# Batch normalization on one core: the first tile's store goes out in two transfers

## The chip, the cores and the metric

The kernel runs on one core of a Trainium2 chip. The metric is the device time of one execution in microseconds (us). Before the change the median of 3 runs is 2484.38 us (2483.38 to 2485.73).

## What is computed

The input `x` is 32 x 256 x 128 x 128 in float32, 536.9 MB. Each of the 256 channels has its own `gamma`, `beta`, `running_mean` and `running_var`:

```python
eps = 1e-5
out = gamma * (x - running_mean) / sqrt(running_var + eps) + beta   # per channel
```

That is one multiplication and one addition per element, `x * scale + shift`, with `scale = gamma / sqrt(var + eps)` and `shift = beta - mean * scale`. Every element is read once from HBM and written once to HBM.

## The kernel before

**Tiles.** A tile holds 128 channels of one image: 128 partitions, each with one row of 128 x 128 = 16384 floats (64 KB). There are 32 x 2 = 64 tiles of 8.4 MB. Three buffers `t0` to `t2` hold them in rotation; tile i lies in buffer i modulo 3 and is transformed in place.

**Queues.** Loads are issued by SyncE (`load`, line 86; its queue is SP, the DMA queue q1). Stores are issued by ScalarE (`store`, line 89; its queue is ACT's, the DMA queue q10). Both queues feed the same 16 DMA engines. Each engine moves 8 of the 128 rows of a tile.

**Start.** Tile 0 is loaded in two halves with the four parameter loads between them (line 103); loads 1 and 2 are issued right behind, as their buffers are free. The parameters are turned and combined into `scale_t` and `shift_t` (lines 108 to 125).

**Loop.** For each tile VectorE transforms the first columns (`apply_vector`, line 66) and ScalarE the rest (`apply_scalar`, line 77). Tile 0 is split in half at column 8192. For the other tiles VectorE does columns 0 to 1696, then 1696 to 14976, and ScalarE the last 1408; the last tile has other bounds. Then the store of the tile is issued.

**What sets the order.** The instructions of each engine stand in the order in which the code writes them (`manual_schedule`); waits follow from what each reads and writes. A load into a buffer waits until the store from that buffer has landed: load i+1 waits for store i-2. `follow` adds two more waits by hand:

- Load i+1 waits for VectorE's first piece of tile i, so that a load starts when the load before has landed.
- ScalarE's piece of tile i (for 0 < i < 62) waits for the store of tile i-1 to land. As store i comes after that piece, one store at a time is under way. `stored` is the transfer it waits for.

The loop writes these as

```python
if NHEAD <= i + 1 < NT:
    follow(load(i + 1), released)
...
part = apply_scalar(i, VHEAD if i == 0 else VLAST if i == last else VMOST, HW)
if 0 < i < NT - 2:
    follow(part, stored)
stored = store(i)
```

Of the kernel before, what the change touches and what calls it, by code (L numbers as in the profile page):

```python
# [1 line left out]

# [4 lines left out]


NBUF = 3
PAD = 936  # L10
NHEAD = 3
VFIRST = 1696
VMOST = 14976
VHEAD = 8192
VLAST = 9216


@with_exitstack
def kernel(
    ctx: ExitStack,  # L20
    tc: tile.TileContext,
    x: bass.AP,
    gamma: bass.AP,
    beta: bass.AP,
    running_mean: bass.AP,
    running_var: bass.AP,
    out: bass.AP,
):
    nc = tc.nc
    eps = 1e-5  # L30
    f32 = mybir.dt.float32

    N, C, H, W = x.shape
    P = nc.NUM_PARTITIONS
    assert C % P == 0
    NCB = C // P
    HW = H * W
    NT = N * NCB
    B = 32
    NQ = P // B  # L40
    NE = 16
    NPAR = 4

    xr = x.rearrange("n (cb p) h w -> (n cb) p (h w)", p=P)
    outr = out.rearrange("n (cb p) h w -> (n cb) p (h w)", p=P)

    params = ctx.enter_context(tc.tile_pool(name="params", bufs=1))
    data = ctx.enter_context(tc.tile_pool(name="data", bufs=1))
    params.tile([P, PAD], f32, name="pad", tag="pad")
    bufs = [data.tile([P, HW], f32, name=f"t{s}", tag=f"t{s}") for s in range(NBUF)]  # L50
    rows = params.tile([B, NPAR * C], f32, name="rows", tag="rows")
    turned = params.tile([B, NPAR * C], f32, name="turned", tag="turned")
    par = params.tile([P, NPAR, NCB], f32, name="par", tag="par")
    eps_t = params.tile([P, 1], f32, name="eps_t", tag="eps")
    std_t = params.tile([P, NCB], f32, name="std_t", tag="std")
    rstd_t = params.tile([P, NCB], f32, name="rstd_t", tag="rstd")
    scale_t = params.tile([P, NCB], f32, name="scale_t", tag="scale")
    ms_t = params.tile([P, NCB], f32, name="ms_t", tag="ms")
    shift_t = params.tile([P, NCB], f32, name="shift_t", tag="shift")

    left, right = slice(0, HW // 2), slice(HW // 2, HW)
    last = NT - 1

    def apply_vector(i, first_col, end):
        t, cb = bufs[i % NBUF], i % NCB
        return nc.vector.tensor_scalar(  # L66
            out=t[:, first_col:end],
            in0=t[:, first_col:end],
            scalar1=scale_t[:, cb : cb + 1],
            scalar2=shift_t[:, cb : cb + 1],  # L70
            op0=mybir.AluOpType.mult,
            op1=mybir.AluOpType.add,
        )

    def apply_scalar(i, first_col, end):
        t, cb = bufs[i % NBUF], i % NCB
        return nc.scalar.activation(  # L77
            out=t[:, first_col:end],
            in_=t[:, first_col:end],
            func=mybir.ActivationFunctionType.Identity,  # L80
            bias=shift_t[:, cb : cb + 1],
            scale=scale_t[:, cb : cb + 1],
        )

    def load(i, rows=slice(0, P), cols=slice(0, HW)):
        return nc.sync.dma_start(out=bufs[i % NBUF][rows, cols], in_=xr[i][rows, cols])  # L86

    def store(i, rows=slice(0, P), cols=slice(0, HW)):
        return nc.scalar.dma_start(out=outr[i][rows, cols], in_=bufs[i % NBUF][rows, cols])

    def follow(inst, ahead):
        tc.add_manual_dep(
            inst.ins,
            ahead.ins.name,
            mybir.DependencyInfo(mybir.DependencyClass.Sync, mybir.DependencyReason.DATA),
            reason="one transfer at a time in each queue, released by the computation",
        )

    with tc.manual_schedule():
        load(0, cols=left)  # L100
        nc.vector.memset(rows[:], 0.0)  # L101
        for r, ap in enumerate((running_var, gamma, beta, running_mean)):
            nc.sync.dma_start(out=rows[0:NE, r * C : (r + 1) * C], in_=ap.partition_broadcast(NE))  # L103
        load(0, cols=right)
        for i in range(1, NHEAD):
            load(i)

        nc.vector.memset(eps_t[:], eps)  # L108
        nc.vector.transpose(out=turned[:], in_=rows[:])  # L109
        blocks = turned.rearrange("p (rc q b) -> p rc q b", q=NQ, b=B)  # L110
        flat = par.rearrange("p r cb -> p (r cb)")
        for q in range(NQ):
            nc.vector.tensor_copy(out=flat[q * B : (q + 1) * B], in_=blocks[:, :, q, 0])  # L113
        var_t, gamma_t, beta_t, mean_t = (par[:, r] for r in range(NPAR))
        nc.scalar.activation(  # L115
            out=std_t[:],
            in_=var_t,
            func=mybir.ActivationFunctionType.Sqrt,
            bias=eps_t[:],
            scale=1.0,  # L120
        )
        nc.vector.reciprocal(out=rstd_t[:], in_=std_t[:])  # L122
        nc.vector.tensor_mul(out=scale_t[:], in0=gamma_t, in1=rstd_t[:])  # L123
        nc.vector.tensor_mul(out=ms_t[:], in0=mean_t, in1=scale_t[:])  # L124
        nc.vector.tensor_sub(out=shift_t[:], in0=beta_t, in1=ms_t[:])  # L125

        stored = None
        for i in range(NT):
            if i == 0:
                apply_vector(i, 0, VHEAD)  # L130
            else:
                released = apply_vector(i, 0, VFIRST)
                if NHEAD <= i + 1 < NT:
                    follow(load(i + 1), released)
                apply_vector(i, VFIRST, VLAST if i == last else VMOST)
            part = apply_scalar(i, VHEAD if i == 0 else VLAST if i == last else VMOST, HW)
            if 0 < i < NT - 2:
                follow(part, stored)
            stored = store(i)


# [1 line left out]
_INS = ['x', 'gamma', 'beta', 'running_mean', 'running_var']  # L143
_OUTS = [((32, 256, 128, 128), 'float32')]


# [23 lines left out]
```

## Time and profile before

| | us |
|---|---|
| median of 3 runs | 2484.38 |
| the profiled execution, whole | 2483.26 |
| its span on the core | 2481.2 |
| VectorE busy | 526.0 |
| ScalarE busy | 111.9 |
| VectorE idle, waiting for loads (line 66) | 1915.2 |
| ScalarE idle, waiting for stores (line 77) | 2271.7 |

The span runs from the first instruction to the last event on the core; the 2.1 us between it and the whole execution lie outside. HBM is read for 536.94 MB and written for 536.87 MB, 433 GB/s over the span. In the timeline a row names its start, its length, the engine ("ACTq" and "SPq" are the queues of ScalarE and SyncE, where transfers are issued), the line and the operation; in brackets stands how long the engine was idle before it and what released it. The landing of a load is read from the VectorE row that it releases, the landing of a store from the ScalarE row. The trace also holds a record of every DMA packet: start, length, bytes, queue.

### The profile page before, as it was taken

Reading aid. Unit: us, or ns where it says so; the run is one execution under the profiler, and the core shown is the slowest. Engines: PE = TensorE matmul, PEld = TensorE weight load, DVE = VectorE, ACT = ScalarE, POOL = GpSimd, SP = SyncE. Lnnn points to the kernel's source line nnn. Section 1 sums busy time; section 2 is a strip of 40 time slices with the busy share of each in tenths; the row PEclk is TensorE's granted clock in tenths of the full one; section 3 lists DMA queues with packets and bytes.
Section 4 is the critical chain, followed back from the end, with each engine's and each line's share of the span. In section 5 each row is a group of like instructions: output and inputs, shape, how many; then the busy total and the mean of one; then the engine's idle time right before and its main releaser. Section 6 shows DMA issues by size and latency. Waiting matters only on the chain.

```text
span 2481.2 us, 695 instructions
## 1 busy us (share of the span) xinstructions
DVE 526.0 (21%) x138; ACT 111.9 (5%) x66; POOL 0.2 (0%) x4
## 2 busy tenths in 40 slices
DVE  2122121221212212122121221212212212122120
ACT  1000000000000000000000000000000000000001
POOL 0000000000000000000000000000000000000000
DMA  9999999999999999999999999999999999999999
GB/s 422 425 438 437 426 437 436 428 437 440 425 437 438 426 436 438 427 437 438 426 437 438 427 437 437 426 438 437 426 440 437 427 437 437 433 431 437 434 429 408
DMA packets 18709, 1073.86 MB, mean 433 GB/s; under 512 B 2128, under 2 KB 2192, under 8 KB 2192
## 3 DMA queue, kind: packets, MB, share of 16 engines
q1 hardware_dynamic: 9488, 536.94, 50.0%
q10 hardware_dynamic: 9216, 536.88, 49.9%
q14 instruction: 5, 0.04, 0.0%
HBM read 536.94 MB, written 536.87 MB: 433 GB/s over the span
## 4 chain that ended last, share of the span: by engine, by line
DMA 94%; DVE 3%; another core or an unknown queue 1%; ACT 0%; issue 0%; SPq 0%; DVEq 0%
DMA t<-in_x_dram 94%; DVE t L66 3%; ACT t L77 0%; SPq L86 0%; SPq L103 0%; DVEq L66 0%; DVE rows L101 0%; DVE eps_t L108 0%
## 5 line engine op out<-in xcount | busy, mean ns | idle before, releaser
L66 DVE TENSOR_SCALAR t<-t,scale_t,shift_t 128x13280 f32<-128x13280 f32 (+2 forms) x127 | 522.6, 4157 | 1915.2 <-DMA t<-in_x_dram 1915.2
L77 ACT ACTIVATE t<-t,shift_t,scale_t 128x1408 f32<-128x1408 f32 (+1 forms) x64 | 110.3, 1723 | 2329.3 <-DMA out_dram<-t 2271.7
L109 DVE STREAM_TRANSPOSE turned<-rows 32x1024 f32<-32x1024 f32 x1 | 1.2, 1232 | 11.9 <-DMA rows<-in_running_mean_dram 11.9
L115 ACT ACT_TABLE_LOAD x1 | 1.3, 1283 | 0.7 <-PEq L154 0.7
L101 DVE MEMSET rows<- 32x1024 f32 x1 | 0.9, 912 | 1.0 <-PEq L154 1.0
L115 ACT ACTIVATE std_t<-par,eps_t 128x2 f32<-128x2 f32 x1 | 0.3, 295 | 13.8 <-DVE par L113 13.8
L113 DVE COPY par<-turned 32x8 f32<-32x8 f32 x4 | 0.6, 161 | 0.1
L122 DVE RECIPROCAL rstd_t<-std_t 128x2 f32<-128x2 f32 x1 | 0.2, 165 | 0.4 <-ACT std_t L115 0.4
L124 DVE TENSOR_TENSOR ms_t<-par,scale_t 128x2 f32<-128x2 f32 x1 | 0.2, 161 | 0.0
L125 DVE TENSOR_TENSOR shift_t<-par,ms_t 128x2 f32<-128x2 f32 x1 | 0.2, 161 | 0.0
L123 DVE TENSOR_TENSOR scale_t<-par,rstd_t 128x2 f32<-128x2 f32 x1 | 0.2, 160 | 0.0
L154 POOL MEMSET const-bfloat16-1.0<- 128x1 bf16 x1 | 0.1, 102 | 0.0
L154 POOL MEMSET const-uint8-127<- 128x1 uint8 x1 | 0.1, 101 | 0.0
L154 POOL MEMSET const-float32-0.0<- 128x1 f32 x1 | 0.1, 98 | 0.2 <-issue 0.2
L154 POOL MEMSET const-float32-1.0<- 128x1 f32 x1 | 0.1, 98 | 0.0
L108 DVE MEMSET eps_t<- 128x1 f32 x1 | 0.1, 59 | 0.0
## 6 DMA issues: line engine op xcount, KB each, us to landing
t<-in_x_dram SPq DMA_DIRECT2D x2, 4096.0 KB, 15.8
out_dram<-t ACTq DMA_DIRECT2D x64, 37.0
t<-in_x_dram SPq DMA_DIRECT2D x63, 37.3
rows<-in_running_var_dram SPq DMA_DIRECT2D x1, 16.0 KB, 11.2
rows<-in_gamma_dram SPq DMA_DIRECT2D x1, 16.0 KB, 11.0
rows<-in_beta_dram SPq DMA_DIRECT2D x1, 16.0 KB, 10.7
rows<-in_running_mean_dram SPq DMA_DIRECT2D x1, 16.0 KB, 10.4
```

Source lines behind the costliest of these rows:

```text
L66: return nc.vector.tensor_scalar(out=t[:, first_col:end], in0=t[:, first_col:end], scalar1=scale_t[:, cb : cb + 1], scalar2=shift_t[:, cb ...
L77: return nc.scalar.activation(out=t[:, first_col:end], in_=t[:, first_col:end], func=mybir.ActivationFunctionType.Identity, bias=shift_t[: ...
L101: nc.vector.memset(rows[:], 0.0)
L108: nc.vector.memset(eps_t[:], eps)
L109: nc.vector.transpose(out=turned[:], in_=rows[:])
L113: nc.vector.tensor_copy(out=flat[q * B : (q + 1) * B], in_=blocks[:, :, q, 0])
L115: nc.scalar.activation(out=std_t[:], in_=var_t, func=mybir.ActivationFunctionType.Sqrt, bias=eps_t[:], scale=1.0,)
L122: nc.vector.reciprocal(out=rstd_t[:], in_=std_t[:])
L123: nc.vector.tensor_mul(out=scale_t[:], in0=gamma_t, in1=rstd_t[:])
L124: nc.vector.tensor_mul(out=ms_t[:], in0=mean_t, in1=scale_t[:])
L125: nc.vector.tensor_sub(out=shift_t[:], in0=beta_t, in1=ms_t[:])
L154: nc = _bacc.Bacc("TRN2", target_bir_lowering=False, num_devices=1)
```

## The change

The store of tile 0 is issued as two transfers: columns 0 to 1024 (128 rows of 4 KB), then columns 1024 to 16384 (128 rows of 60 KB). The wait of ScalarE's piece of tile 1 follows the second. All other stores stay whole. Lines behind the new constant move down by one.

```diff
+LEAD = 1024
...
-            stored = store(i)
+            if i == 0:
+                store(i, cols=slice(0, LEAD))
+                stored = store(i, cols=slice(LEAD, HW))
+            else:
+                stored = store(i)
```

Columns 0 to 1024 are written by VectorE alone; the second transfer holds columns of VectorE and of ScalarE. Load 3, which goes into the buffer of tile 0, waits for both transfers.

## The prediction

> **What bounds the kernel now.** I read the page's lines of transfer rates, then the timeline of the first tiles and of a late one, then the packet records that lie under the DMA rows of the trace (start, length, bytes and queue of every packet).
>
> ```profile
> span 2481.2 us, 695 instructions
> ...
> DMA  9999999999999999999999999999999999999999
> GB/s 422 425 438 437 426 437 436 428 437 440 425 437 438 426 436 438 427 437 438 426 437 438 427 437 437 426 438 437 426 440 437 427 437 437 433 431 437 434 429 408
> ...
> q1 hardware_dynamic: 9488, 536.94, 50.0%
> q10 hardware_dynamic: 9216, 536.88, 49.9%
> ```
>
> The 16 DMA engines are full in every slice; the loads (q1) and the stores (q10) each take half. The compute engines are nowhere near: DVE is busy 526.0 us, ACT 111.9. The packet records say how full. A row of a tile (65536 bytes) is one packet of 2.414 us; the records form 16 chains, each record ending where the next begins; each chain holds 1032 data packets worth 1024 whole rows, and 1024 x 2.4143 = 2472.2 us. After 20 us I find no gap over 0.05 us in any chain. So 2472.2 of the span's 2481.2 us is moving bytes, and 9.0 us is the rest: 2.1 before the first packet, 0.9 after the last, some 6 of stretched packets. A change can win at most a few us here; it can lose whatever it lets the engines stand empty.
>
> What keeps them full is when the two queues pause:
>
> ```profile
> 0.73 0.37 SPq L86 DMA_DIRECT2D t<-in_x_dram  x1
> ...
> 23.29 7.21 ACT L77 ACTIVATE t<-t,shift_t,scale_t 128x8192 f32<-128x8192 f32 x1 [7.20 <-DMA t<-in_x_dram]
> 30.53 0.38 ACTq L89 DMA_DIRECT2D out_dram<-t  x1
> 52.74 8.27 DVE L66 TENSOR_SCALAR t<-t,scale_t,shift_t 128x1696 f32<-128x1696 f32 x2 [31.29 <-DMA t<-in_x_dram]
> 74.63 1.56 ACT L77 ACTIVATE t<-t,shift_t,scale_t 128x1408 f32<-128x1408 f32 x1 [44.13 <-DMA out_dram<-t]
> 76.22 0.34 ACTq L89 DMA_DIRECT2D out_dram<-t  x1
> 84.39 8.27 DVE L66 TENSOR_SCALAR t<-t,scale_t,shift_t 128x1696 f32<-128x1696 f32 x2 [23.37 <-DMA t<-in_x_dram]
> ...
> 113.91 1.56 ACT L77 ACTIVATE t<-t,shift_t,scale_t 128x1408 f32<-128x1408 f32 x1 [37.72 <-DMA out_dram<-t]
> 115.50 0.34 ACTq L89 DMA_DIRECT2D out_dram<-t  x1
> 123.72 8.27 DVE L66 TENSOR_SCALAR t<-t,scale_t,shift_t 128x1696 f32<-128x1696 f32 x2 [31.06 <-DMA t<-in_x_dram]
> ```
>
> An ACT row starts when the store before has landed (74.63: store 0; 113.91: store 1); a DVE row starts when a load has landed (84.39: load 2; 123.72: load 3). So store i lands 9.8 us **before** load i+2, and late in the run still (ACT 2395.79, DVE 2405.54). In the pause of the stores the loads have the engines, in the pause of the loads the stores. One engine's packets in order (L a load's row, s a store's), from 22.6 us:
>
> ```
> LLLLL sLsLsL ss LsLsLs LLLLL ssss LsLsLsLs LLLL ssss LsLsLsLs
> ```
>
> Four rows of each alone, eight alternating. Two things are seen here. Both queues waiting, they take **turns packet by packet**. And the 4-byte packet that raises the semaphore takes a whole turn: load 1 has its eighth row, a store's row follows, then the load's semaphore packet, then again a store's row: the "ss". Its cost shows too: the last row of load 1 ended at 50.31 us, its last semaphore packet at 52.72, one packet later.
>
> **The change, part by part.** Nothing is removed. Store 0 becomes 128 rows of 4096 bytes and 128 rows of 61440: for each engine 8 small packets, a semaphore packet, 8 large ones, a semaphore packet.
>
> *Added work.* 4 KB at the same rate is 0.15 us, and 8 x 0.15 + 8 x 2.26 is what 8 whole rows took. The parameter rows (1024 bytes) took 46 ns where their bytes make 38, so 8 ns a packet: under 0.1 us for 8. A second issue on ACT's queue costs 0.4 us (30.53 0.38), with nothing behind it but the activation of tile 1, which waits for the store until after 70 us. Nothing.
>
> *An earlier start.* In the order of the changed kernel's instructions the small store waits for the vector half alone, not for the activation ahead of it; the large one waits for the activation. The trace of before shows no issue beside a running ACTIVATE, so it leaves between 23.3 us (when that ACTIVATE starts) and 30.5. I take the early end, since the wait is all that held the store; both lead to the same place below.
>
> *The turns.* This decides. Before, store 0 took 8 turns of rows and one of its semaphore against the loads' turns. Now it takes 8 + 1 + 8 + 1, and 9 of them move nearly nothing. Count for one engine. Load 1's rows begin at 22.5 to 23.3 us. In before, the store issued at 30.53 had its first packet at 35.28 us at the earliest: one load row was still chosen ahead. A lead issued at 23.3 so comes first after two rows of load 1, at 27.3 to 28.1. Load turns left: 6 rows of load 1, its semaphore, 8 rows of load 2: 15. The small rows and their semaphore use 9 of these; the large rows meet the last 6; then come the seventh large row, load 2's semaphore, the eighth large row. So store 0 lands one row, 2.3 us, **after** load 2. With the late issue (first packet at 35.3, 5 rows of load 1 gone) the same count leaves 4 large rows behind load 2's semaphore: 9.1 us after. Before it was 9.8 us ahead. When it lands is fixed by bytes: 8 + 8 + 8 rows from 22.5 to 23.3 us are 24 x 2.414 = 57.9 us, so 80.4 to 81.2, and with the stretch at the first store packet (load rows of 3.1 to 3.6 us near 32 us) up to 82; before, 74.6.
>
> *What is late next.* Load 3 goes into tile 0's buffer, so it waits for store 0; so does the activation of tile 1, by the pacing, and with it store 1. Both queues are empty when store 0 lands, and the engines stand still until load 3's first packet. Load 3 starts at once, store 1 after 1.56 us of ACT. The load so has two rows before the first store row, keeps that lead through the alternation, and lands before store 1. Load 4 waits for store 1 by its buffer, store 2 by the pacing: again one event frees both. Nothing in the loop undoes it, as the load always ends first and always waits. Stores 0 to 60 each release such a pair (loads 3 to 63): **61 pauses**.
>
> *Price of a pause.* No row of before shows an empty engine between tiles. The nearest is the start: issue at 0.73, first packet at 2.11 (1.38 us). The first half rows took 1.8 to 2.0 us where later ones took 1.21, so 0.6 more. From landing to issue 0.1 us (the ACT starts 0.04 us after store 0's last semaphore packet, SP issues 0.06 us after the DVE's release at 85.56). Sum 0.1 + 1.38 + 0.6 = 2.08 us. From below: 0.05 + 1.38 with no slow first row, 1.43. From above: a late load, issued at 2406.78 with its first packet at 2410.72, is 3.94 us less the row chosen ahead (2.41), 1.53; with 0.15 to issue, 0.8 for the slow row, and 0.74 by which the engines' first packets spread at the start (2.11 to 2.85): 3.22. I take 2.08, the start's own rows. A gain has no place in a pause.
>
> *Sum.* 61 x 2.08 = 126.9 us, on the profiled execution's 2483.26 us (span 2481.2 and 2.1 around it; 1.1 below the median 2484.38): 2610.1. Ends: 61 x 1.43 = 87 gives 2570, 61 x 3.22 = 196 gives 2680.
>
> **The rivals.** *The lead takes one turn, not nine.* If an engine passed all 8 small rows at a stroke, store 0 would be delayed by one or two turns at 2.41 us and start up to 7 us earlier: it would land some 5 us or more before load 2, the pauses would lie apart as now, and nothing would stand still: 2483.3, and within 0.2% (5 us, about what a measurement of this kernel can tell from no change). The same holds if turns were shared by bytes, since store 0 then has the bytes it had. For it: no row of before shows small data rows of one queue beside another. Against: whole rows alternate singly, and a packet of 4 bytes took a full turn, at the end of every transfer. It decides if store 0 lands 4 us or more ahead of load 2.
>
> The Trainium skill ("DMA: Bandwidth & Descriptors", section Queues, rings and completion order) speaks for this rival: an engine is to drain a whole packet, typically 9 to 17 descriptors, from one ring before it turns to the next. The lead's 8 rows and semaphore on an engine are 9 descriptors; by that rule they are one turn and the time stays. The trace disagrees for whole rows, which are nine descriptors too and change queue at every one; no run here shows it for 4 KB rows.
>
> *A near miss.* If the lead gets two more turns than I count, store 0 lands just before load 2. Then the store has the two rows of advance: they cover most of its own pause and the load's. At 0 to 0.3 us for 61 tiles: 2483 to 2502. Against: in before two of the 16 engines let the first store packet in one row later than the others, never earlier, and the slowest engine decides.
>
> *The change does less than it says:* the lead goes out only at 30.5. Priced above: the same pauses.
>
> **How the numbers follow.** Locked pauses 0.80 (2610, 2570 to 2680); one turn or by bytes 0.14 (2483); near miss 0.06 (half within 0.2%, half slower). Slower 0.83, same 0.16, faster 0.01. The range is that of the first case; what it leaves out is 0.20.
>
> **What would show it.** Right: in the timeline the DVE row of load i+2 starts two to five us before the ACT row of store i, from load 2 on (79 against 82 us); SP waits for stores 61 times; a step from tile to tile is 40.7 us in place of 38.63; the rate over the span falls to about 412 GB/s; each chain of packets shows some 2 us empty per tile. A lead that leaves at 23.3 confirms the missing wait. Wrong: store 0 landing well before load 2, with steps of 38.63; or the order turned but pauses under 1.4 us, which would mean that an empty engine starts faster than at the kernel's start.

## The result, and the profile after

The changed kernel takes 2721.2 us (median of 5 runs, 2715.7 to 2727.03) against 2484.38 us: ratio 1.0952, 95% interval 1.0935 to 1.0969. The profiled execution has a span of 2718.9 us. The direction and the course of events were as forecast; the time lies above the range (2570 to 2680).

The page of the changed kernel, the lines that answer to those shown of before:

```profile
span 2718.9 us, 697 instructions
...
DMA  9999999999999999999999999999999999999999
GB/s 420 383 401 387 400 400 371 417 386 401 400 371 416 378 394 400 373 415 386 401 399 387 402 386 401 386 386 401 386 417 386 386 401 394 408 386 386 401 386 417
...
q1 hardware_dynamic: 9488, 536.94, 49.4%
q10 hardware_dynamic: 9360, 536.88, 45.6%
```

The row of busy tenths still shows 9 everywhere: a loss of 4 us in 42 is below its resolution. The engines stand empty for about 2.3 us of it; the rest is rows that take too long and still count as busy. The rate tells it, 371 to 417 GB/s in every slice after the first (395 over the span), where most slices had 425 to 440 (433). So the loss is not an event near the start, where the only edited transfer is, but something that goes on to the end.

The timeline of the first tiles of the changed kernel (start, length, engine, line, operation; in brackets the idle time before and what ended it):

```profile
23.24 7.21 ACT L78 ACTIVATE t<-t,shift_t,scale_t 128x8192 f32<-128x8192 f32 x1 [6.89 <-DMA t<-in_x_dram]
23.26 7.56 ACTq L90 DMA_DIRECT2D out_dram<-t  x2
43.65 8.27 DVE L67 TENSOR_SCALAR t<-t,scale_t,shift_t 128x1696 f32<-128x1696 f32 x2 [21.93 <-DMA t<-in_x_dram]
79.21 8.27 DVE L67 TENSOR_SCALAR t<-t,scale_t,shift_t 128x1696 f32<-128x1696 f32 x2 [27.29 <-DMA t<-in_x_dram]
81.67 1.56 ACT L78 ACTIVATE t<-t,shift_t,scale_t 128x1408 f32<-128x1408 f32 x1 [51.22 <-DMA out_dram<-t]
83.26 0.34 ACTq L90 DMA_DIRECT2D out_dram<-t  x1
122.39 8.27 DVE L67 TENSOR_SCALAR t<-t,scale_t,shift_t 128x1696 f32<-128x1696 f32 x2 [34.92 <-DMA t<-in_x_dram]
124.69 1.56 ACT L78 ACTIVATE t<-t,shift_t,scale_t 128x1408 f32<-128x1408 f32 x1 [41.46 <-DMA out_dram<-t]
```

The two ACT-queue issues stand in one row that begins at 23.26: the lead left as soon as the ACTIVATE had begun. Then the order is turned round. Load 2 lands at 79.2 and store 0 at 81.7 (before: 84.4 and 74.6), load 3 at 122.4 and store 1 at 124.7. ACT starts 43.0 us after its last start, where it was 39.3 and later 38.6 us.

Who waits for whom on SyncE's queue, first in the kernel before, then in the changed one (waiting time in all, times, longest):

```profile
SPq L86 <- DVE t L66: 1711.4, 61, 72.2
SPq L86 <- DMA out_dram<-t: 655.1, 24, 27.9
```

```profile
SPq L87 <- DMA out_dram<-t: 2595.1, 61, 67.9
```

Before, each of the 61 later loads waited for VectorE's first piece, that is, for the landing of the load before it; 24 of them stood at a store as well. Now each of the 61 waits for a store alone. The same store lets go ScalarE, and so the next store:

```profile
ACT t L78 <- DMA out_dram<-t: 2513.1, 61, 51.2
```

One event, two queues, 61 times. Stretches from one landing of a store to the next show what a tile costs, before and after (start and end, length, busy times, DMA share, GB/s):

```profile
230.80:269.40 38.60, 8.27 (x2) 1.56 (x1) 0.00 (x0) 1.00 1.00 433
```

```profile
252.19:294.51 42.32, 8.35 (x3) 1.56 (x1) 0.00 (x0) 1.00 0.96 396
```

The packet records give the anatomy of the loss. A record doesn't name its engine; the records form 16 chains in which each begins where the one before it ends, and a chain is taken as an engine. Times of single packets are given here, as in the prediction, some 0.4 us later than recorded, so that the last semaphore packet of a store ends where the row that it releases starts; lengths and distances don't depend on it. One engine from 23 us (L load row, s store row, "4" a 4 KB store row, "|" an empty engine):

```
LL 4L4L4L4L4L4L 44 LL sLsLsLsLsLsL ss | LL sLsLsLsLsLsL ss | LL s
```

Each 4 KB row (0.16 us) takes a turn against a 64 KB load row (2.42 us), and the semaphore packet of load 1 takes one too (the "44"). From there every tile is two load rows, alternation, and an empty engine. Each of the 16 engines has exactly 61 such gaps, before had none. On average over all of them the engine is empty for 2.28 us, the first load row after it is 0.65 us too long, and the second load row, after which the store joins, 1.01 us. Sum 3.94 us; 61 x 3.94 = 240 us, and the spans differ by 237.7.

### The profile page after: what moved, and what is told of

It is laid out like the page before. It is cut to its first block, busy times and chain, and to the rows that moved or that the text cites. A ratio compares the mean times of both kernels' runs of the same rounds, so it can differ in the third digit from the quotient of the medians.

```text
span 2718.9 us, 697 instructions
## 1 busy us (share of the span) xinstructions
DVE 526.0 (19%) x138; ACT 111.9 (4%) x66; POOL 0.2 (0%) x4
## 4 chain that ended last, share of the span: by engine, by line
DMA 93%; ACT 4%; another core or an unknown queue 1%; issue 0%; SPq 0%; DVE 0%; ACTq 0%
DMA out_dram<-t 90%; ACT t L78 4%; DMA t<-in_x_dram 3%; SPq L104 0%; DVE rows L102 0%; ACTq L78 0%; SPq L87 0%; DVE eps_t L109 0%
```

## The experiments

The theory is that of the prediction: turns go by packets, the nine extra turns of store 0 put its landing behind load 2's, and from then on one landing frees both queues. The rivals put the cost into the split itself: a second transfer that shifts the round of completion semaphores, small rows that move badly, or sharing by bytes.

### Split without extra turns (e1_rows)

```diff
-                store(i, cols=slice(0, LEAD))
-                stored = store(i, cols=slice(LEAD, HW))
+                store(i, rows=slice(0, 16))
+                stored = store(i, rows=slice(16, P))
```

> Store 0 still goes out in two transfers, but split by rows: partitions 0 to 16, then 16 to 128, each row whole. Turn theory: an engine has 1 row, a semaphore packet, 7 rows, a semaphore packet: one turn more than before and not nine. Store 0 lands at about 77 us, some 6 us before load 2, the pauses of the queues stay apart, steps of 38.63 us: 2484 us, within 0.2%. Rival (the second transfer as such does it, by one more completion semaphore that shifts all later ones round by one, or one more issue): slow as with the change, 2715 to 2727.

2492.03 us, ratio 1.0026 (1.0016 to 1.0036). The second transfer and its semaphore are there, and the 237 us are not:

```profile
85.19 1.56 ACT L77 ACTIVATE t<-t,shift_t,scale_t 128x1408 f32<-128x1408 f32 x1 [54.58 <-DMA out_dram<-t]
...
93.16 8.27 DVE L66 TENSOR_SCALAR t<-t,scale_t,shift_t 128x1696 f32<-128x1696 f32 x2 [27.04 <-DMA t<-in_x_dram]
```

Store 0 landed at 85.2 us, load 2 at 93.2: the order of before, with steps of 38.67 us. But both are 9 to 11 us later than in the kernel before, and store 0 is 8 us later than I expected: the 16 rows of the first part took 3.4 to 8.5 us each where a row takes 2.42. From store 1 on the stores land 8.5 to 9.4 us behind those of before, so the delay, 7 us in the medians, is paid once. A second thing is in it: the two landings lie only 8.0 us apart here, and 12 of the 16 engines stood empty once, for 0.4 to 4.9 us, just after store 0 had landed.

The Trainium skill ("SBUF — State Buffer", section Door 1: The DMA port swizzle) offers a cause for the slow rows: a transfer's rate depends on how many of the 16 ports its partitions reach, and partitions 0 to 15 reach four. Four rows to a port would be 4 x 2.41 = 9.7 us as an estimate from that page's map; from the start of the first of these rows to the end of the last the records show 9.3 us, which agrees. No other run here varies the partitions, so the cause isn't tested further.

### A late lead, and a wide one (e2_late, e3_half)

```diff
-                store(i, cols=slice(0, LEAD))
-                stored = store(i, cols=slice(LEAD, HW))
+                store(i, cols=slice(HW - LEAD, HW))
+                stored = store(i, cols=slice(0, HW - LEAD))
```

> The lead is the last 1024 columns, which ScalarE writes, so it can't leave before 30.5 us. Turn theory: first small packet at about 35.3 us, load 2 lands at 72 to 74 us, store 0 at 81 to 82 us (some 9 us later, where the change has 2.4), and from there the same 61 pauses of 3.9 us: 2715 to 2727. Rival (it is the early start that brings the order to the brink; a late lead leaves store 0 ahead): under 2500.

```diff
-LEAD = 1024
+LEAD = 8192
```

> The lead is 8192 columns (rows of 32 KB, then rows of 32 KB). Turn theory: the number of turns is that of the change, 8 + 1 + 8 + 1, so store 0 lands at 81 to 82 us behind load 2 again: 2715 to 2727. Rival (small rows move badly, or turns go by bytes): with 32 KB rows little of it is left, 2484 to 2520.

2723.35 us and 2722.8 us (one run each). The late lead was issued at 30.5 us; load 2 landed at 72.7 and store 0 at 81.7, 9 us later:

```profile
72.69 8.27 DVE L67 TENSOR_SCALAR t<-t,scale_t,shift_t 128x1696 f32<-128x1696 f32 x2 [21.20 <-DMA t<-in_x_dram]
81.73 1.56 ACT L78 ACTIVATE t<-t,shift_t,scale_t 128x1408 f32<-128x1408 f32 x1 [51.23 <-DMA out_dram<-t]
```

The wide lead: load 2 at 81.45, store 0 at 82.65. Neither the early start nor the small rows matter. What the two kernels share with the change is the count of turns and the order of the landings, and store 0 lands about where the bytes of 24 rows put it in all three.

### The loads get the same handicap (e4_load2)

```diff
-        for i in range(1, NHEAD):
-            load(i)
+        load(1)
+        load(2, cols=slice(0, LEAD))
+        load(2, cols=slice(LEAD, HW))
```

> As the change, and load 2 is split in the same way into columns 0 to 1024 and the rest, so that the loads have nine turns more too. Turn theory: from the first store packet on, the loads have 6 + 1 + 8 + 1 + 8 + 1 turns against the stores' 18; store 0 lands at about 68 to 71 us, load 2 at 81 to 93, the order is that of before and nothing stands still: 2480 to 2490. Rival (a split transfer costs by itself): at least as slow as the change, 2720 or more.

A second split transfer takes nearly all of the loss of the first away: 2500.97 us (2486.27 to 2505.39, 10 runs), ratio 1.0046 (1.0024 to 1.0069), though the median lies 11 us above the 2490 that I allowed.

```profile
67.89 1.56 ACT L78 ACTIVATE t<-t,shift_t,scale_t 128x1408 f32<-128x1408 f32 x1 [37.32 <-DMA out_dram<-t]
...
91.73 8.27 DVE L67 TENSOR_SCALAR t<-t,scale_t,shift_t 128x1696 f32<-128x1696 f32 x2 [39.20 <-DMA t<-in_x_dram]
```

Store 0 lands at 67.9 us, load 2 at 91.7. That is now farther ahead than is of use at the end: the profiled execution (2489.47 us) has one standstill of 5.2 us per engine near 2462 us, where the last store but one is through and the last tile is still being computed. Six of the ten runs lie at 2500 to 2505 us; what they lose besides is not shown, as none of them was profiled.

### One wait less (e5_free32, e6_free1, e10_free12)

The condition ahead of `follow(part, stored)` is changed, in the three kernels in this order:

```diff
-            if 0 < i < NT - 2:
+            if 0 < i < NT - 2 and i != 32:
+            if 1 < i < NT - 2:
+            if 2 < i < NT - 2:
```

> As the change, but the activation of tile 32, and of it alone, doesn't wait for store 31. Store 32 then stands in the queue behind store 31, and the landing of store 31 frees only load 34: the engines have store 32's rows meanwhile, and from there the stores are ahead again. Turn theory: steps of 42.6 us up to store 30's landing (31 pauses of 3.9 us, 122 us on 2483), then steps of 38.6 to 39.2 us: 2603 to 2625. Rival (every tile is slow for a reason of its own, whatever the order of the two landings): 2715 to 2727.

> As the change, but the activation of tile 1 doesn't wait for store 0, so that store 1 stands behind store 0 when load 2 has landed. Turn theory: store 0 still lands at 81 to 82 us and load 2 before it, but no pause follows: 2483 to 2520, with steps of 38.6 to 39.2 us. Rival: as the change, 2715 to 2727.

2649.46 us for the first (one run), 2573.21 us for the second (ratio 1.0363, 1.0348 to 1.0379). The first runs in steps of 42.6 us (on average) up to the tile where the wait is gone and in steps of 39.2 and 41.5 us behind it; the second has such steps from the start. So the steps of 42.6 us are a state that lasts until something turns it, and not a property of a tile. But both times lie above what I expected, which was steps of 38.6 to 39.2. The timeline of the second shows what is left:

```profile
156.85 1.56 ACT L78 ACTIVATE t<-t,shift_t,scale_t 128x1408 f32<-128x1408 f32 x1 [37.59 <-DMA out_dram<-t]
...
161.66 8.27 DVE L67 TENSOR_SCALAR t<-t,scale_t,shift_t 128x1696 f32<-128x1696 f32 x2 [32.70 <-DMA t<-in_x_dram]
198.28 1.56 ACT L78 ACTIVATE t<-t,shift_t,scale_t 128x1408 f32<-128x1408 f32 x1 [39.86 <-DMA out_dram<-t]
...
200.71 8.27 DVE L67 TENSOR_SCALAR t<-t,scale_t,shift_t 128x1696 f32<-128x1696 f32 x2 [30.78 <-DMA t<-in_x_dram]
237.72 1.56 ACT L78 ACTIVATE t<-t,shift_t,scale_t 128x1408 f32<-128x1408 f32 x1 [37.88 <-DMA out_dram<-t]
...
242.62 8.27 DVE L67 TENSOR_SCALAR t<-t,scale_t,shift_t 128x1696 f32<-128x1696 f32 x2 [33.64 <-DMA t<-in_x_dram]
```

The store lands first again, but by 2.4 to 4.9 us and not by 9.8; steps alternate between 39.2 and 41.5 us (mean 40.13). That is too little. In the kernel before, a queue needs some 7 to 10 us from the last row of a transfer to the first row of the next, its turnaround: the last row of store 60 ended at 2393.34, the first rows of store 61 on the engines began at 2400.73 to 2402.99, 7.4 to 9.7 us later; over the run it is 7.0 to 9.7 us for the stores and 7.4 to 10.5 for the loads. Where the two queues' turnarounds begin much less than that apart, they overlap, and the engines empty. So order would be half of the condition and distance the other half. The next run tests that by letting two stores queue up:

> As the change, but the activations of tiles 1 and 2 don't wait for the store before. With one of them freed the landings turned round, but only by 3 to 4 us, and a pause of 1.5 us a tile was left. Distance theory: a queue's turnaround, from its last row to the first row of its next transfer, is 7 to 10 us, so nothing stands still only if the landings lie about 10 us apart, as in the kernel before (9.8). Two stores queued ahead give the stores a second turnaround of the loads, some 3 to 4 rows more: distance 10 to 13 us, steps of 38.63 us, 2483 to 2492. Rival (the split start leaves a lasting cost that no order removes): about 2570, as with one.

2484.23 us, ratio 1.0001 (0.9992 to 1.001). With the split still in place the whole loss is gone:

```profile
79.36 8.27 DVE L67 TENSOR_SCALAR t<-t,scale_t,shift_t 128x1696 f32<-128x1696 f32 x2 [27.54 <-DMA t<-in_x_dram]
...
153.00 1.56 ACT L78 ACTIVATE t<-t,shift_t,scale_t 128x1408 f32<-128x1408 f32 x1 [72.08 <-DMA out_dram<-t]
...
163.11 8.27 DVE L67 TENSOR_SCALAR t<-t,scale_t,shift_t 128x1696 f32<-128x1696 f32 x2 [31.67 <-DMA t<-in_x_dram]
192.06 1.56 ACT L78 ACTIVATE t<-t,shift_t,scale_t 128x1408 f32<-128x1408 f32 x1 [37.51 <-DMA out_dram<-t]
...
201.77 8.27 DVE L67 TENSOR_SCALAR t<-t,scale_t,shift_t 128x1696 f32<-128x1696 f32 x2 [30.39 <-DMA t<-in_x_dram]
```

Load 2 is at 79.4, as in the changed kernel (79.2); by the next landings shown the store is 10.1 us ahead, then 9.7, and stays there, and no engine stands empty between tiles.

### The same order without any split (e11_wait)

```diff
-        for i in range(1, NHEAD):
-            load(i)
+        heads = [load(i) for i in range(1, NHEAD)]
...
             stored = store(i)
+            if i == 0:
+                follow(stored, heads[0])
```

> The kernel before, store 0 whole, but its issue waits for load 1 to land (about 42 us, as the loads then have the engines alone). No extra turn and no second transfer. Order theory: first store row at 46 to 47 us, 9 turns against some 7 of load 2, so store 0 lands at 81 to 82 us behind load 2 (about 79), one event frees both queues, 61 pauses of 3.9 us follow: 2715 to 2730. Rival (the change is slow because of the split itself, its small rows or its extra completion semaphore): a late start costs nothing or its 12 us once, 2484 to 2500.

2722.23 us (one run). No split, no small rows, no extra semaphore, and a time within 1.1 us of the changed kernel's median:

```profile
42.63 0.37 ACTq L89 DMA_DIRECT2D out_dram<-t  x1
79.30 8.27 DVE L66 TENSOR_SCALAR t<-t,scale_t,shift_t 128x1696 f32<-128x1696 f32 x2 [28.47 <-DMA t<-in_x_dram]
81.71 1.56 ACT L77 ACTIVATE t<-t,shift_t,scale_t 128x1408 f32<-128x1408 f32 x1 [51.16 <-DMA out_dram<-t]
```

This settles it: the order of two landings at 79 and 82 us is worth 237 us, however it comes about.

### What the pause is made of (e8_act, e9_act8)

In the first kernel, and in the second:

```diff
-VMOST = 14976
+VMOST = 12288
+VMOST = 8192
```

> As the change, with ScalarE doing 4096 columns of a tile in place of 1408 (about 3.8 us in place of 1.56), so that a store joins some 2.2 us, about one row, later after each pause. If the second row after a pause is stretched by 1.0 us because the stores join there, the stretch moves to the third row and the pause stays at 3.9 us: 2710 to 2735. If the first two rows after a standstill are slow whoever joins, the second row stays stretched, with the same time. Third possibility: the stretch goes, 2.9 us a pause, about 2660.

> As the run with 4096 columns, but 8192 (7.2 us): a store joins after about four load rows, as late in a tile as it does in the kernel before, where its first row stretches nothing. If the joining stretches whatever row it meets, the fourth or fifth row is stretched by 1.0 us, 2710 to 2735. If it needs the loads to have just started again, no row but the first is stretched, 2.9 us a pause, about 2660.

2725.33 and 2722.59 us (one run each); 42.65 and 42.60 us a step. In the first the stretched row is the third (1.14 us on average, the second 0.02), in the second the fourth (1.14), in both the one just ahead of the first store row. So the stretch belongs to the joining store and not to the load's second row. It doesn't need loads that have just begun, but it goes with a standstill: in the kernel before, stores join behind four or five load rows 964 times over the 16 engines with 0.00 to 0.01 us of stretch on average; here after four rows, behind a standstill, the average is 1.14. In these kernels the loads come back first: their first row is 0.65 us too long, and the return of the stores costs another 1.0 to 1.1 on the load row ahead of it.

It isn't the same when the stores come back first. In e6_free1 an engine stands empty for over 0.5 us (0.85 on average) 336 times over the 16 engines, each time with a store's row next: that row is only 0.03 us too long, and the price falls on the return of the loads, 0.71 us on the store's row ahead of it and 1.24 on the first load row.

Why an engine that was empty pays a second time when the other queue joins is not settled; what it does inside is not in the records. Nor is the gap on the engine itself the whole rule: in e6_free1 the first row of a store is 0.57 us too long on average in the 645 cases where its own engine shows no gap over 0.05 us ahead of it.

## Why the prediction was right in its course and wrong in its size

- *What bounds the kernel; nothing to win.* Right. The best of the other kernels equals the time before.
- *Added work: nothing.* Right: 8 rows of 0.16 us.
- *An earlier start.* Right: the issues begin at 23.26 us. It is worth nothing (e2_late).
- *The turns.* Right in each count: first lead row at 27.4 to 28.0 us on 14 engines, one row later on two (expected 27.3 to 28.1); two rows of load 1 before them, six and a semaphore turn of load 1 between, store 0 landing at 81.7 us (80.4 to 82), 2.5 us after load 2 (2.3). The rule of the Trainium skill that spoke for the first rival ("DMA: Bandwidth & Descriptors", section Queues, rings and completion order) would have left the time at 2483, with one turn for 9 descriptors; the trace shows a change of queue at every 4 KB row, so the measurement decides against it here.
- *What is late next; 61 pauses.* Right: 61 on every engine, 61 waits of SyncE for stores.
- *The price of a pause, 2.08 us with an upper end of 3.22.* **This step failed**: it is 3.94. By its terms: from a landing to the first packet it had 0.1 + 1.38 = 1.48, and the runs show 1.43; for the slow first row it had 0.6, and they show 0.65. Missing from the sum are the engines' spread (on average an engine ended 0.63 us before the last landing and started 0.22 us after the first packet, together 0.85) and the stretch of 1.01 us where the store joins. I had both rows in hand: the load rows near 32 us (2.5 to 3.6 us by the records, not 3.1 to 3.6) were counted once, as an event of the kernel's start. They stand just ahead of the first store row after the start, where the engines had been empty too; e8_act and e9_act8 show that such a stretch belongs to the store that joins behind a standstill, and a pause repeats it. The spread I put into the upper end alone. 1.43 + 0.65 + 0.85 + 1.01 = 3.94, and 2483.3 + 61 x 3.94 = 2723.6 would have been the forecast.
- *The near miss.* It was not what happened, but e6_free1 shows that I had it wrong as well: I priced two rows of advance at 0 to 0.3 us a tile; there the store is one to two rows ahead, and it costs 1.5. I had taken the turnaround of a queue for two rows; it is three to four.

## What to carry to other kernels

Where two queues share the DMA engines and each allows one transfer at a time, look at the order of their landings and at the distance between them. Here nothing was lost in the rounds with 9.7 us and more between them, about a turnaround of a queue; a distance of 8.0 us emptied most engines once; 2.4 to 4.9 us cost 1.5 us a tile, and a load 2.4 us ahead of the store that frees both queues 3.9 us. Where between 4.9 and 9.7 us a lasting loss begins was not measured. Such an order can be a lasting state, set by one transfer at the start: count turns, one per row and one per semaphore packet, before splitting it. And when a standstill is new, price it with all that the first standstill of the trace cost, the second queue's restart too.

## What the runs showed of the hardware

- An engine with two queues waiting changes queue at every row, whether of 4 KB, 32 KB, 60 KB or 64 KB, and the 4-byte semaphore packet at a transfer's end takes a whole turn (the changed kernel and e3_half).
- After a standstill the two queues come back at a cost. Loads first: 0.65 us on the first load row, 1.0 to 1.1 us on the load row ahead of the first store row. Stores first (e6_free1): 0.03 us on the first store row, 0.71 us on the store row ahead of the first load row, 1.24 us on that load row. In the kernel before, where nothing stands still, a joining queue costs 0.00 to 0.03 us on average.
- A transfer of 16 neighbouring rows of 64 KB took 9.3 us, its rows 3.4 to 8.5 us each where 2.42 is usual; the rate over the stretch from 30 to 40 us was 282 GB/s (e1_rows).
